# A hybrid transformer layer on one core: the Hyena filter's norm as a factor per channel, taps' sums from summed weights, and w_down's products of the FFN by halves of the columns

## The chip, the core and the metric

The kernel runs on one core of a Trainium2 chip. The core has a matmul engine (PE, with PEld for its weight loads), a vector engine (DVE), a scalar engine (ACT), a general engine (POOL), and SP, which here only issues transfers. The metric is the device time of one execution in microseconds; smaller is better. Products are kept near float32 by splitting every operand into a high and a low part and adding three matmuls (`mm3`); each split costs one ACT cast and one subtraction on DVE or POOL.

## The reference

Two layers over a stream x (512 tokens, width 1024) and a context stream (256 tokens). Each layer mixes x by attention, a Fourier mix and a Hyena long convolution, and then runs a gated FFN with a short convolution. In layer 0 the context is updated too. The parts that the change touches:

```python
def hyena_filter(L, w1, b1, fr1, w2, b2, fr2, w3):
    ...
    h = jnp.sin(fr1 * (z @ w1 + b1))
    h = jnp.sin(fr2 * (h @ w2 + b2))
    h = h @ w3                                   # L x 512: forward and backward taps
    h_fwd, h_bwd = h[:, :256] * decay, h[:, 256:] * decay
    two = jnp.concatenate([h_fwd, zeros, h_bwd[:0:-1]], axis=0)
    return two / jnp.sum(jnp.abs(two), axis=0, keepdims=True)

def hyena_longconv(u, filt, bias):               # by FFT of length 2L
    return irfft(rfft(u) * rfft(filt)) + u * bias

def hyena_mix(p, conv_w, conv_b, filt, bias):
    x0, x1, v = jnp.split(dwconv3(p, conv_w, conv_b), 3, axis=-1)
    return x0 * hyena_longconv(x1 * v, filt, bias)

def conv_ffn(h, w_up, w_c, b_c, w_down):
    gate, val = jnp.split(dwconv3(h @ w_up, w_c, b_c), 2, axis=-1)
    return (jax.nn.silu(gate) * val) @ w_down    # 2816 -> 1024
```

## The kernel before

The program is written as Python generators that a small list scheduler interleaves (`go` runs the main stage, `add` puts side work into lanes, `pump` steps side work by its due time, with costs such as `C512` and waits from the table `Z`). A framework then orders the instructions of each engine; that order is fixed in the program. On each engine instructions run strictly in order, and a wait holds up all that stand behind it.

**Hyena filters.** There are three: `c` (context, layer 0), `x0` and `x1` (x in layers 0 and 1). All three are side work: `c` runs in the first 45 us beside the loads of w_mod, and `x0` and `x1` run between about 45 and 245 us beside the input projections. `filter_taps` makes two sines (`sine`, tiles `taps`, `sn`) and then, for each tile of 128 taps, one product with w3 into PSUM, the multiplication by `decay` (`dec`), an absolute value (`fab`), a running sum of it on POOL, and sum and difference of the forward and backward halves (`fsd`), which are split into `sd`. At the end two matmuls with ones add the norm over all taps (line 792), and `inv` is its reciprocal, 128x256. `filter_spectrum` multiplies each transformed block by `inv` (`keo`), and adds and subtracts to make `K`, which goes to DRAM. `hyena` later multiplies the spectra and transforms back.

**FFN of x** (`ffn_x`). 22 column tiles m of w_up. Each takes seven products of half size (a Strassen-like scheme: `first` makes two, `rest` five; 84 matmuls of 256 columns). `prep` loads w_up (tiles `r`), POOL forms four differences (`tt`), and ACT and DVE split them (`Wh`, `Wl`, `w`). The convolution (`ft`), silu and the gate's product give `gT`, one tile per m. The m's go in nine groups of two and a last group of four. While group i runs, after its first m, `ffn_down` adds the products of group i−1 with w_down: it loads two row tiles of w_down, 128x1024 each (`Wr`, two buffers), splits them, makes 12 matmuls of 512 columns for each of the four token tiles into one PSUM tile of 1024 columns (`pw`, two buffers), and DVE adds that to `y` (line 1228; ACT copies it in the first group). The last group also does the norm and the residual (`tail`, `residual`, `norm_pre`).

```python
                if i and j == 0:
                    yield from self.ffn_down(l, st, g, groups[i - 1], i == 1)
```

In the rows below, `pn` and `pw` are PSUM tiles, `h` parts of the normed x, `Wh`/`Wl` split weights, `gT` split gates, `p`/`nmax` the attention's exponentials and row maxima, `rd_y` a reciprocal root for a norm.

## Time and profile before

| | |
|---|---|
| median of three runs (lowest, highest) | 1776.45 us (1773.36, 1780.07) |
| the profiled execution, its span | 1779.94 us, 1778.2 us |
| busy: PE, DVE, ACT, POOL | 1645.9, 1428.7, 932.4, 690.6 us |
| mean granted PE clock | 0.973 |
| context filter; filters of x; FFN of x, layer 0; FFN of x, layer 1 | about 10–42, 45–245, 700–1080, 1395–1774 us |

A page of the profile shows one execution. Busy times are shares of the span, so an average over stages with different limits; what a change in one stage is worth must be read from that stage. A row of a timeline gives start, duration, engine, line, operation, tiles, and in brackets how long the engine had stood idle and what released it. PE's matmuls are pipelined: a matmul of 256 columns is shown with 0.28 us, and one starts every 0.12 us.

### The profile page before, as it was taken

Reading aid. Unit: us, or ns where it says so; the run is one execution under the profiler, and the core shown is the slowest. Engines: PE = TensorE matmul, PEld = TensorE weight load, DVE = VectorE, ACT = ScalarE, POOL = GpSimd, SP = SyncE. Lnnn points to the kernel's source line nnn. Section 1 sums busy time; section 2 is a strip of 40 time slices with the busy share of each in tenths; the row PEclk is TensorE's granted clock in tenths of the full one; section 3 lists DMA queues with packets and bytes.
Section 4 is the critical chain, followed back from the end, with each engine's and each line's share of the span. In section 5 each row is a group of like instructions: output and inputs, shape, how many; then the busy total and the mean of one; then the engine's idle time right before and its main releaser. Section 6 shows DMA issues by size and latency. Waiting matters only on the chain. (4 is left out here: it accounts for less than half of the span.)

```text
span 1778.2 us, 27879 instructions
## 1 busy us (share of the span) xinstructions
PE 1645.9 (93%) x10534; PEld 1401.5 (79%) x10534; DVE 1428.7 (80%) x2291; ACT 932.4 (52%) x1741; POOL 690.6 (39%) x515
## 2 busy tenths in 40 slices
...
GB/s 348 121 60 147 93 236 273 224 13 139 166 252 227 229 151 83 83 119 85 106 142 84 95 184 314 201 175 119 1 48 83 131 145 105 97 105 87 125 64 119
DMA packets 70003, 248.01 MB, mean 139 GB/s; under 512 B 8111, under 2 KB 9647, under 8 KB 69868
## 3 DMA queue, kind: packets, MB, share of 16 engines
...
## 5 line engine op out<-in xcount | busy, mean ns | idle before, releaser
L196 PE MATMUL pn<-h,Wh 128*128 128x256 f32 x1328 | 376.4, 286 | 9.6 <-ACT Wh L181 3.4
L198 PE MATMUL pn<-h,Wl 128*128 128x256 f32 x1328 | 372.3, 284 | 10.0 <-DVE Wl L182 9.9
L197 PE MATMUL pn<-h,Wh 128*128 128x256 f32 x1328 | 374.0, 283 | 1.7 <-POOL h L182 1.7
L196 PEld LDWEIGHTS pn<-h,Wh 128*128 128x128 f32 x1328 | 252.7, 191 | 22.0 <-issue 4.8
L198 PEld LDWEIGHTS pn<-h,Wl 128*128 128x128 f32 x1328 | 251.7, 191 | 14.7 <-DVE Wl L182 12.1
L197 PEld LDWEIGHTS pn<-h,Wh 128*128 128x128 f32 x1328 | 253.5, 191 | 6.2 <-POOL h L182 2.4
L181 ACT CAST Wh<-Wr 128x1024 fp32r<-128x1024 f32 x118 | 122.7, 1048 | 139.1 <-PE pn L197 44.7
L182 DVE TENSOR_TENSOR Wl<-Wr,Wh 128x1024 fp32r<-128x1024 f32 x89 | 130.0, 1468 | 54.0 <-ACT Wh L181 46.4
L1302 POOL TENSOR_TENSOR tt<-r,r 128x512 f32<-128x512 f32 x44 | 73.2, 1664 | 236.4 <-DMA r<-w_up 223.4
L196 PE MATMUL pw<-Wh,gT 128*128 128x512 f32 x352 | 137.4, 403 | 9.0 <-ACT gT L181 3.8
L197 PE MATMUL pw<-Wl,gT 128*128 128x512 f32 x352 | 138.1, 395 | 3.3 <-DVE Wl L182 3.3
L198 PE MATMUL pw<-Wh,gT 128*128 128x512 f32 x352 | 137.9, 396 | 1.8 <-DVE gT L182 1.7
L181 ACT CAST Wh<-tt 128x1024 fp32r<-128x1024 f32 x88 | 90.8, 1048 | 81.8 <-PE pn L197 39.0
L182 DVE TENSOR_TENSOR Wl<-tt,Wh 128x1024 fp32r<-128x1024 f32 x88 | 121.0, 1394 | 12.3 <-ACT Wh L181 10.0
L1361 POOL TENSOR_TENSOR ft<-ft,ft 128x512 f32<-128x512 f32 x44 | 70.7, 1608 | 133.5 <-DVE ft L658 94.8
L1228 DVE TENSOR_TENSOR y<-y,pw 128x1024 f32<-128x1024 f32 x82 | 99.3, 1213 | 18.1 <-PE pw L198 18.0
L182 POOL TENSOR_TENSOR h<-tf,h 128x256 fp32r<-128x256 f32 (+1 forms) x40 | 35.0, 893 | 183.3 <-ACT h L181 182.0
L182 POOL TENSOR_TENSOR Wl<-Wr,Wh 128x1024 fp32r<-128x1024 f32 x29 | 72.6, 2508 | 59.6 <-ACT Wh L181 59.2
L1304 POOL TENSOR_TENSOR tt<-r,tt 128x512 f32<-128x512 f32 x44 | 75.8, 1722 | 47.6 <-DVE Wl L182 47.6
L656 ACT ACTIVATE ft<-C,vec 128x512 f32<-128x512 f32 x88 | 68.7, 811 | 36.7 <-DVE C L1351 27.4
L196 PE MATMUL pw<-h,Wh 128*128 128x256 f32 (+1 forms) x224 | 76.1, 340 | 12.7 <-DVE y L1228 2.6
L294 PE MATMUL pn<-wm,cpad 128*32 128x256 f32 x768 | 70.3, 427 | 16.8 <-DMA wm<-w_mod 16.2
...
## 6 DMA issues: line engine op xcount, KB each, us to landing
wm<-w_mod SPq DMA_DIRECT2D x96, 512.0 KB, 5.0
r<-w_up SPq DMA_DIRECT2D x90, 512.0 KB, 3.7
Wr<-w_down SPq DMA_DIRECT2D x66, 512.0 KB, 4.2
L<-w_up SPq DMA_DIRECT2D x44, 512.0 KB, 4.4
Wr<-w_out SPq DMA_DIRECT2D x24, 512.0 KB, 3.6
Wr<-w_in_t SPq DMA_DIRECT2D x16, 512.0 KB, 4.5
dft<-hdft_x POOLq DMA_DIRECT2D x16, 512.0 KB, 4.4
Wr<-w_in_c SPq DMA_DIRECT2D x12, 512.0 KB, 3.6
```

Source lines behind the costliest of these rows:

```text
L181: r = nc.scalar.copy(hi, src)
L182: (el or nc.vector).tensor_tensor(lo, src, f32(hi), op=ALU.subtract)
L196: nc.tensor.matmul(ps, l[0], r[0], start=first, stop=False, **kw)
L197: nc.tensor.matmul(ps, l[0], r[1], start=False, stop=False, **kw)
L198: nc.tensor.matmul(ps, l[1], r[0], start=False, stop=last, **kw)
L294: nc.tensor.matmul(ps[32 * g : 32 * g + 32, cs], self.cpad[:, q % 2 * 4 + g, :], w[:, g, :], start=q % 2 == 0, stop=q % 2 == 1, skip_group ...
L656: nc.scalar.activation(dst, ps, AF.Identity, scale=w1, bias=b)
L1228: nc.vector.tensor_tensor(y, y, acc[t], op=ALU.add)
L1302: te.tensor_tensor(half(t13, 0), half(r[1], 0), half(r[0], 0), op=ALU.subtract)
L1304: te.tensor_tensor(half(t24, 0), half(r[1], 1), half(t13, 0), op=ALU.subtract)
L1361: nc.gpsimd.tensor_tensor(o[0], o[0], o[1], op=ALU.mult)
```

## The change

It has two parts.

*Filter.* w3's two halves become their sum and difference once (DVE, 64x256 each), so that the matmul gives sum and difference of the taps directly, and one multiplication by a decay of 256 columns makes `fsd`. The absolute values for the norm come from max(|sum|, |difference|) (ACT makes the absolute values, DVE the maximum, POOL adds 256 columns instead of 512). The norm is taken per channel as a column (two matmuls with one moving column each) and is no longer multiplied into the spectrum: `hyena` applies 1/norm as a factor per channel in its last step, and bias times norm in the step before. `K` comes straight from PSUM, with one ACT copy and two DVE steps. A sine scales by 1/2π in an ACT step with scale and bias, rounds in two DVE steps, and calls Sin with a scale.

*FFN of x.* `down_half` takes one half of w_down's columns for both k of a group: one load of 128x2x512, 24 matmuls into two PSUM tiles, each of which holds two token tiles, and two sums. `Z['HV']` says after which m of a group each half stands: the first half after the first m, the second after the second; in group 1 both after the first; in the last group after its second and its fourth m. `y` is now a tile for two token tiles and one half of the columns. The residual is written into `xr`, and in layer 0 the norm's result into two halves.

```diff
+Z = {'HV': [[[0], [1]], [[0, 1], []], [[], [0], [], [1]]], 'go_mod00': 1.0, ...}   (the other entries as before)
...
         for k in range(4):
-            src = x[:, (4 * b + k) * P : (4 * b + k + 1) * P]
+            src = x[b][:, k * P : (k + 1) * P] if isinstance(x, list) else x[:, (4 * b + k) * P : (4 * b + k + 1) * P]
...
         else:
-            self.nc.scalar.activation(n, x, AF.Copy, scale=r)
+            for d, v in zip(n, (x[:, 0:512], x[:, 512:1024])) if isinstance(n, list) else [(n, x)]:
+                self.nc.scalar.activation(d, v, AF.Copy, scale=r)
...
     def sine(self, a, ps, b, fr):
-        nc = self.nc
-        T = a.shape[1]
-        n = self.T(T, "sn", parts=64)
-        nc.vector.tensor_scalar(a, ps, b, fr, op0=ALU.add, op1=ALU.mult)
-        nc.vector.tensor_scalar(n, a, 1.0 / TWO_PI, ROUND, op0=ALU.mult, op1=ALU.add)
-        nc.vector.tensor_scalar(n, n, -ROUND, None, op0=ALU.add)
-        for c in (CW1, CW2):
-            nc.vector.scalar_tensor_tensor(a, n, -c, a, op0=ALU.mult, op1=ALU.add)
-        nc.vector.tensor_scalar(a, a, PI_LO, -PI_LO, op0=ALU.min, op1=ALU.max)
-        nc.scalar.activation(a, a, AF.Sin)
+        nc = self.nc
+        n = self.T(a.shape[1], "sn", parts=64)
+        nc.scalar.activation(a, ps, AF.Identity, scale=fr, bias=b)
+        nc.vector.tensor_scalar(n, a, ROUND, None, op0=ALU.add)
+        nc.vector.scalar_tensor_tensor(a, n, ROUND, a, op0=ALU.subtract, op1=ALU.subtract)
+        nc.scalar.activation(a, a, AF.Sin, scale=-2.0 * PI_LO)
...
+        nc.vector.tensor_scalar(hw[:, 2:4], hw[:, 2:4], 1.0 / TWO_PI, None, op0=ALU.mult)
+        nc.vector.tensor_tensor(hw[:, 0:2], hw[:, 0:2], hw[:, 2:4], op=ALU.mult)
+        ws, wd = w3[:, 0:256], w3[:, 256:512]
+        nc.vector.tensor_tensor(ws, ws, wd, op=ALU.add)
+        nc.vector.scalar_tensor_tensor(wd, wd, -2.0, ws, op0=ALU.mult, op1=ALU.add)
...
-                    nc.gpsimd.dma_start(win2, I["decay_" + st.name][t // 2])
-            win = win2[:, t % 2]
-            dec = self.T(512, "dec")
-            nc.vector.tensor_tensor(dec, ps, win, op=ALU.mult)
-            ab = acc if t == 0 else self.T(512, "fab")
-            nc.vector.scalar_tensor_tensor(ab, dec, -1.0, dec, op0=ALU.mult, op1=ALU.max)
+                    nc.gpsimd.dma_start(win2, I["decay_" + st.name][t // 2, :, :, 0:256])
+            f = self.half2("fsd")
+            nc.vector.tensor_tensor(f, ps.rearrange("p (s d) -> p s d", s=2), win2[:, t % 2].unsqueeze(1).broadcast_to([P, 2, 256]), op=ALU.mult)
+            if t == 0:
+                nc.vector.tensor_tensor(f[0:1, 0], f[0:1, 0], f[0:1, 1], op=ALU.add)
+                nc.scalar.activation(f[0:1, 1], f[0:1, 0], AF.Copy, scale=0.5)
+                nc.scalar.activation(f[0:1, 0], f[0:1, 0], AF.Copy, scale=0.5)
+            ab = self.T(256, "fab") if t else acc
+            fa = self.half2("fa")
+            nc.scalar.activation(fa, f, AF.Abs)
+            nc.vector.tensor_tensor(ab, fa[:, 0], fa[:, 1], op=ALU.max)
...
-            f = self.half2("fsd")
-            nc.vector.tensor_tensor(f[:, 0, :], dec[:, 0:256], dec[:, 256:512], op=ALU.add)
-            nc.gpsimd.tensor_tensor(f[:, 1, :], dec[:, 0:256], dec[:, 256:512], op=ALU.subtract)
...
-        for e in range(2):
-            nc.tensor.matmul(ps[:, 0:256], self.ones.broadcast_to([P, P]), acc[:, e * 256 : (e + 1) * 256], start=e == 0, stop=e == 1)
-        o["inv"] = inv = acc[:, 0:256]
-        nc.vector.reciprocal(inv, ps[:, 0:256])
-        nc.vector.tensor_scalar(inv, inv, 1.0 / st.T, None, op0=ALU.mult)
-        yield CF512, 3.0
+        for m in range(2):
+            nc.tensor.matmul(ps[:, m : m + 1], acc[:, m * P : (m + 1) * P], self.ones, start=True, stop=True)
+        nrm = self.small("fnorm", 4, 3)
+        nc.vector.tensor_scalar(nrm[:, 2:4], ps[:, 0:2], float(st.T), None, op0=ALU.mult)
+        nc.vector.reciprocal(nrm[:, 0:2], nrm[:, 2:4])
+        nc.vector.tensor_tensor(nrm[:, 2:4], nrm[:, 2:4], self.vec[l][:, V_HB : V_HB + 2], op=ALU.mult)
+        o["norm"] = nrm
+        yield 0.4, 3.0
...
-                eo = self.half2("keo")
-                nc.vector.tensor_tensor(eo, ps.rearrange("p (e d) -> p e d", e=2), inv.unsqueeze(1).broadcast_to([P, 2, 256]), op=ALU.mult)
-                nc.vector.tensor_tensor(Kt[:, s, 0, :], eo[:, 0], eo[:, 1], op=ALU.add)
-                self.kp = nc.gpsimd.tensor_tensor(Kt[:, s, 1, :], eo[:, s], eo[:, 1 - s], op=ALU.subtract).ins
+                eo = self.T(256, "keo")
+                nc.scalar.copy(eo, ps[:, 256:512])
+                nc.vector.tensor_tensor(Kt[:, s, 0, :], ps[:, 0:256], eo, op=ALU.add)
+                if s == 0:
+                    self.kp = nc.vector.tensor_tensor(Kt[:, 0, 1, :], ps[:, 0:256], eo, op=ALU.subtract).ins
+                else:
+                    self.kp = nc.vector.scalar_tensor_tensor(Kt[:, 1, 1, :], ps[:, 0:256], -1.0, eo, op0=ALU.mult, op1=ALU.add).ins
...
-                nc.vector.scalar_tensor_tensor(t_, u[m][:, par : st.T : 2], vec[:, V_HB + m : V_HB + m + 1], ps[:, m * H : (m + 1) * H], op0=ALU.mult, op1=ALU.add)
-                nc.vector.tensor_tensor(self.mixf(st, 6 + m)[:, par : st.T : 2], t_, st.x0[m][:, par : st.T : 2], op=ALU.mult)
+                nc.vector.scalar_tensor_tensor(t_, u[m][:, par : st.T : 2], nrm[:, 2 + m : 3 + m], ps[:, m * H : (m + 1) * H], op0=ALU.mult, op1=ALU.add)
+                nc.vector.scalar_tensor_tensor(self.mixf(st, 6 + m)[:, par : st.T : 2], t_, nrm[:, m : m + 1], st.x0[m][:, par : st.T : 2], op0=ALU.mult, op1=ALU.mult)
...
-            nc.vector.scalar_tensor_tensor(y[:, hs], y[:, hs], r, x[:, hs], op0=ALU.mult, op1=ALU.add)
+            if isinstance(y, list):
+                nc.vector.scalar_tensor_tensor(x[:, hs], y[h], r, x[:, hs], op0=ALU.mult, op1=ALU.add)
+            else:
+                nc.vector.scalar_tensor_tensor(y[:, hs], y[:, hs], r, x[:, hs], op0=ALU.mult, op1=ALU.add)
...
-        if begin and st is self.X:
-            st.y = [self.M("y", F32) for _ in range(st.NT)]
-        wd = {k: self.load_w(self.I["w_down"][l, k], el=nc.gpsimd if el else None) for k in ms}
+        if st is self.X:
+            ww = [[self.load_down(l, k, h) for k in (ms[0], ms[2])] for h in range(2)]
+            W = lambda k, h: tuple(v[:, (k - ms[0]) % 2] for v in ww[h][(k - ms[0]) // 2])
+            st.y = [[st.Y[h][t // 2][:, t % 2 * 512 : t % 2 * 512 + 512] for h in range(2)] for t in range(st.NT)]
+        else:
+            wd = {k: self.load_w(self.I["w_down"][l, k], el=nc.gpsimd if el else None) for k in ms}
+            W = lambda k, h: tuple(v[:, h * 512 : (h + 1) * 512] for v in wd[k])
...
             for k in ks:
-                self.mm3(acc[t, h], (g[k][:, 0, ts], g[k][:, 1, ts]), (wd[k][0][:, hs], wd[k][1][:, hs]), k == ms[0], k == ms[-1])
+                self.mm3(acc[t, h], (g[k][:, 0, ts], g[k][:, 1, ts]), W(k, h), k == ms[0], k == ms[-1])
...
                 if end:
-                    nc.vector.tensor_tensor(y[:, hs], y[:, hs], acc[t, h], op=ALU.add)
-                    self.sumsq_half(ss[t], y[:, hs], h)
-                    nc.gpsimd.tensor_tensor(y[:, hs], y[:, hs], st.G[1][:, hs], op=ALU.mult)
+                    v = y[h] if st is self.X else y[:, hs]
+                    nc.vector.tensor_tensor(v, v, acc[t, h], op=ALU.add)
+                    self.sumsq_half(ss[t], v, h)
+                    nc.gpsimd.tensor_tensor(v, v, st.G[1][:, hs], op=ALU.mult)
...
+    def load_down(self, l, k, h):
+        return self.load_w(self.I["w_down"][l, k : k + 2, :, h * 512 : (h + 1) * 512].rearrange("k p c -> p k c"), [P, 2, 512])
+    def down_half(self, l, st, g, ms, h):
+        nc = self.nc
+        if ms[0] == 0:
+            if h == 0:
+                st.Y = [[], []]
+            st.Y[h] = [self.M("y", F32) for _ in range(st.NT // 2)]
+        w = self.load_down(l, ms[0], h)
+        for i, y in enumerate(st.Y[h]):
+            ps = self.pw()
+            for t in range(2):
+                ts = slice((2 * i + t) * P, (2 * i + t + 1) * P)
+                for k in range(2):
+                    v = g[ms[k]]
+                    self.mm3(ps[:, t * 512 : t * 512 + 512], (v[:, 0, ts], v[:, 1, ts]), (w[0][:, k], w[1][:, k]), k == 0, k == 1)
+                yield 6 * C512, 0.0
+            if ms[0] == 0:
+                nc.scalar.copy(y, ps)
+            else:
+                nc.vector.tensor_tensor(y, y, ps, op=ALU.add)
...
-                if i and j == 0:
-                    yield from self.ffn_down(l, st, g, groups[i - 1], i == 1)
+                if i:
+                    for h in Z["HV"][1 if i == 1 else 2 if i == len(groups) - 1 else 0][j]:
+                        yield from self.down_half(l, st, g, groups[i - 1], h)
...
                 if last:
-                    nc.sync.dma_start(self.out[t], st.y[t])
+                    nc.sync.dma_start(self.out[t], xr)
                 else:
-                    nc.sync.dma_start(self.dr["x2"][t], st.y[t])
-                    n = self.norm_diag(st.y[t], xr) if Z["DG"][2] >> t & 1 else self.norm_pre(st.y[t], xr, False, RT)
+                    nc.sync.dma_start(self.dr["x2"][t], xr)
+                    n = self.norm_diag(xr, st.y[t]) if Z["DG"][2] >> t & 1 else self.norm_pre(xr, st.y[t], False, RT)
```

The framework's order moves with it. Three places:

On ACT, the start of layer 0's attention, where the last steps of the context's residual (`rd_y`, casts `Wh` of w_out tiles) stand beside the first exponentials `p`. Before:

```order
L1001 ACTIVATE p_3334,den_3335<-pw_3327,nmax_3332 128x768
L224 ACT_TABLE_LOAD
L224 ACTIVATE rd_y_3239<-ss_3043,rd_x_3237 128x1
L181 CAST Wh_4249<-Wr_4247 128x1024
L181 CAST Wh_4279<-Wr_4277 128x1024
L233 ACTIVATE junk_3310,ss_3044<-pn_3285 128x512
L224 ACTIVATE rd_y_3315<-ss_3044,rd_x_3313 128x1
L181 CAST Wh_4318<-Wr_4316 128x1024
L181 CAST Wh_4398<-Wr_4396 128x1024
L1001 ACT_TABLE_LOAD
L1001 ACTIVATE p_3344,den_3335<-pw_3337,nmax_3342 128x768
L1001 ACTIVATE p_3353,den_3335<-pw_3346,nmax_3351 128x768
```

and now:

```order
L222 ACT_TABLE_LOAD
L222 ACTIVATE rd_y_3238<-ss_3042,rd_x_3236 128x1
L1014 ACT_TABLE_LOAD
L1014 ACTIVATE p_3333,den_3334<-pw_3326,nmax_3331 128x768
L179 CAST Wh_4248<-Wr_4246 128x1024
L179 CAST Wh_4278<-Wr_4276 128x1024
L231 ACTIVATE junk_3309,ss_3043<-pn_3284 128x512
L222 ACT_TABLE_LOAD
L222 ACTIVATE rd_y_3314<-ss_3043,rd_x_3312 128x1
L179 CAST Wh_4317<-Wr_4315 128x1024
L1014 ACT_TABLE_LOAD
L1014 ACTIVATE p_3343,den_3334<-pw_3336,nmax_3341 128x768
```

The fourth cast stands behind the next exponentials now, and there are two more table loads.

On DVE, one pair of m's in the steady part of layer 1's FFN (`Wl<-Wr` is a w_down tile, `y` the sums). Before:

```order
L1349 TENSOR_TENSOR C_15955<-C_15955,pn_15970 128x256
L1351 TENSOR_TENSOR C_15926<-pn_15927,C_15926 128x256
L1352 TENSOR_TENSOR C_15955<-pn_15927,C_15955 128x256
L1326 TENSOR_TENSOR C_16130<-C_16130,pn_16132 128x256
L182 TENSOR_TENSOR Wl_16065<-Wr_16062,Wh_16064 128x1024
L182 TENSOR_TENSOR Wl_16071<-Wr_16068,Wh_16070 128x1024
```

and now:

```order
L1278 TENSOR_TENSOR y_14697<-y_14697,pw_15731 128x1024
L1278 TENSOR_TENSOR y_14698<-y_14698,pw_15745 128x1024
L180 TENSOR_TENSOR Wl_15872<-tt_15865,Wh_15871 128x1024
L1397 TENSOR_TENSOR C_15759<-pn_15760,C_15759 128x256
L1398 TENSOR_TENSOR C_15788<-pn_15760,C_15788 128x256
L180 TENSOR_TENSOR gT_15720<-ft_15712,gT_15720 128x512
L180 TENSOR_TENSOR w_15875<-r_15858,w_15875 128x512
L180 TENSOR_TENSOR Wl_15898<-Wr_15895,Wh_15897 128x1024
```

The two w_down tiles of a group stood together; now each stands alone, behind the two sums of the half before it.

On SP's queue, where the w_down loads stand between the w_up loads. Before:

```order
L189 DMA Wr_8637<-w_down 128x1024
L189 DMA Wr_8643<-w_down 128x1024
L1295 DMA r_8599<-w_up 128x1024
L1295 DMA r_8600<-w_up 128x1024
L1295 DMA r_8862<-w_up 128x1024
```

and now:

```order
L187 DMA Wr_8636<-w_down 128x2x512
L1341 DMA r_8599<-w_up 128x1024
L1341 DMA r_8809<-w_up 128x1024
L187 DMA Wr_8847<-w_down 128x2x512
L1341 DMA r_8810<-w_up 128x1024
```

The loads alternate now, one w_down tile for each m.

More of the change, by code (lines that the diff above doesn't have):

```diff
@@ L30 @@
 ROUND = 12582912.0
-CW1 = 6.28125
-CW2 = float(TWO_PI - CW1)
 PI_LO = 3.1415925
@@ L754, in filter_taps @@
         w1, w2, w3 = hw[0:33, 4:68], hw[:, 68:132], hw[:, 132:644]
+        nc.vector.tensor_scalar(hw[:, 2:4], hw[:, 2:4], 1.0 / TWO_PI, None, op0=ALU.mult)
[3 more added lines that the diff above has]
+        nc.vector.scalar_tensor_tensor(wd, wd, -2.0, ws, op0=ALU.mult, op1=ALU.add)
         src, w = zT, w1
         keep = self.M("taps", F32)
-        acc = keep[:, 0:512]
+        acc = keep[:, 0:256]
         for j in range(2):
@@ L770, in filter_taps @@
             if t % 2 == 0:
[L771 removed]
+                win2 = self.Ld(512, "win").rearrange("p (t d) -> p t d", t=2)
                 with self.behind_c() if st is self.X else nullcontext():
[L773 to L778 removed]
+                    nc.gpsimd.dma_start(win2, I["decay_" + st.name][t // 2, :, :, 0:256])
[9 more added lines that the diff above has]
+            nc.vector.tensor_tensor(ab, fa[:, 0], fa[:, 1], op=ALU.max)
             if t:
                 nc.gpsimd.tensor_tensor(acc, acc, ab, op=ALU.add)
[L781 to L783 removed]
             yield 0.0, Z["tp1"]
@@ L800, in filter_spectrum @@
         half = st.NT // 2
-        sd, inv = o["sd"], o["inv"]
+        sd = o["sd"]
+        keep["norm"] = o["norm"]
         for ft in range(half):
```

9 lines of the change are left out of this document (4 added, 5 removed).

## The prediction

> **What bounds the kernel now.** I read the page's first block, then a table of busy time by stage, then every pause of the matmul engine (PE) in order of time.
>
> ```profile
> PE 1645.9 (93%) x10534; PEld 1401.5 (79%) x10534; DVE 1428.7 (80%) x2291; ACT 932.4 (52%) x1741; POOL 690.6 (39%) x515
> 0.00:45.00 45.00, 28.77 (x186) 12.69 (x186) 21.97 (x62) 13.75 (x26) 12.75 (x21) 1.00 0.92 346
> 45.00:250.00 205.00, 189.39 (x992) 151.75 (x992) 165.70 (x331) 85.50 (x206) 85.50 (x92) 0.97 0.40 124
> 250.00:350.00 100.00, 84.22 (x593) 63.93 (x591) 69.30 (x153) 47.52 (x118) 14.88 (x19) 0.95 0.76 253
> 740.00:900.00 160.00, 148.24 (x969) 133.63 (x968) 141.12 (x184) 94.35 (x151) 89.39 (x54) 0.98 0.36 112
> 900.00:1060.00 160.00, 155.82 (x1086) 142.59 (x1085) 144.18 (x161) 83.65 (x131) 80.89 (x54) 1.00 0.36 111
> 1480.00:1750.00 270.00, 266.43 (x1840) 245.88 (x1840) 251.56 (x278) 144.09 (x225) 136.18 (x82) 1.00 0.33 103
> ```
>
> After the stretch and its length stand the busy times of PE, PEld, DVE, ACT and POOL, then clock, DMA share and GB/s. PE is the bound, and no change to DVE or ACT is worth more than PE's pauses in its stage: 16.2 us in the start, 15.6 in 45–250 (where the Hyena filters of both layers run), 15.8 in 250–350, 11.8 and 4.2 in layer 0's FFN of x, 3.6 in the steady part of layer 1's. DVE is close behind PE in the FFN (251.6 of 270 us), so its lateness makes the pauses. These are the pauses that count (start, duration, instruction, in brackets the pause and its releaser):
>
> ```profile
> 18.54 1.11 PE L760 MATMUL pn<-taps,hw 64*64 64x256 f32 x2 [5.97 <-ACT taps L729]
> 114.33 0.35 PE L196 MATMUL pw<-h,Wh 128*128 128x256 f32 x1 [1.19 <-DVE rs_y L216]
> 141.81 0.47 PE L196 MATMUL pw<-h,Wh 128*128 128x512 f32 x1 [2.15 <-DVE v L658]
> 241.23 0.50 PE L196 MATMUL pn<-fd,f 128*128 128x512 f32 x1 [1.78 <-DVE cw L182]
> 350.07 0.79 PE L994 MATMUL pw<-KDup,Q 128*128 128x512 f32 x1 [6.78 <-ACT p L1001]
> 787.18 0.50 PE L197 MATMUL pw<-Wl,gT 128*128 128x512 f32 x1 [2.48 <-DVE Wl L182]
> 820.62 0.73 PE L196 MATMUL pw<-Wh,gT 128*128 128x512 f32 x2 [1.93 <-ACT gT L181]
> 892.19 1.22 PE L196 MATMUL pw<-Wh,gT 128*128 128x512 f32 x2 [2.21 <-ACT Wh L181]
> 912.74 0.38 PE L198 MATMUL pn<-h,Wl 128*128 128x256 f32 x1 [0.64 <-DVE Wl L182]
> 916.21 0.39 PE L198 MATMUL pn<-h,Wl 128*128 128x256 f32 x1 [0.80 <-DVE Wl L182]
> 1097.86 1.12 PE L361 MATMUL pn<-ident,xr 128*128 128x128 f32 x4 [1.77 <-ACT xr L379]
> 1476.88 0.38 PE L198 MATMUL pn<-h,Wl 128*128 128x256 f32 x1 [1.94 <-DVE Wl L182]
> ```
>
> **The change, part by part.** The profiled execution took 1779.94 us (span 1778.2), 3.5 above the median 1776.45; I work out a difference and take it from the median.
>
> Durations in the filter (ns, minimum/median/maximum):
>
> ```profile
> L723 DVE TENSOR_SCALAR taps<-pn,hw x6: 535/794/802, 11.4 to 170.4; 64x512 f32<-64x512 f32 x4, 64x256 f32<-64x256 f32 x2
> L724 DVE TENSOR_SCALAR sn<-taps x6: 278/409/419, 16.2 to 172.9; 64x512 f32<-64x512 f32 x4, 64x256 f32<-64x256 f32 x2
> L727 DVE SCALAR_TENSOR_TENSOR taps<-sn,taps x12: 406/673/686, 16.8 to 176.2; 64x512 f32<-64x512 f32 x8, 64x256 f32<-64x256 f32 x4
> L729 ACT ACTIVATE taps<-taps x6: 416/624/633, 18.1 to 179.2; 64x512 f32<-64x512 f32 x4, 64x256 f32<-64x256 f32 x2
> L778 DVE SCALAR_TENSOR_TENSOR fab<-dec x7: 673/691/1231, 31.0 to 221.0; 128x512 f32<-128x512 f32 x7
> L782 DVE TENSOR_TENSOR fsd<-dec x10: 404/412/2485, 26.8 to 221.7; 128x256 f32<-128x256 f32 x10
> L783 POOL TENSOR_TENSOR fsd<-dec x10: 724/744/1227, 26.3 to 221.9; 128x256 f32<-128x256 f32 x10
> L808 DVE TENSOR_TENSOR keo<-pn,taps x10: 676/682/692, 37.9 to 242.3; 128x512 f32<-128x512 f32 x10
> L794 DVE RECIPROCAL taps<-pn x3: 1748/1750/1757, 35.7 to 230.6; 128x256 f32<-128x256 f32 x3
> 33.76 1.86 PE L792 MATMUL pn<-taps,ones 128*128 128x256 f32 x4
> 136.85 1.03 PE L792 MATMUL pn<-taps,ones 128*128 128x256 f32 x4
> 35.46 0.60 PE L315 MATMUL pn<-ident,mods 128*128 128x128 f32 x4
> ```
>
> *A, the start (filter of the context).* PE stands 5.97 us for the first sine. Of the six DVE steps of a sine, two stay (like L724 and one L727) and one moves to ACT; four of 256 elements go, and DVE no longer interleaves them with the norms: 0.28+0.41+0.41+0.28 = 1.4 us sooner. The norm's ones-products, 1.86 us, become two matmuls with one moving column. None like it is in the trace; it costs over nothing and below the 0.60 of the four small ones at L315, and I take 0.4, so 1.4 is saved. PE hardly pauses between 18.5 and 42 us, so both count: −2.8. Ends: 0, if the w_mod transfers (0.92 of the DMA engines busy) end the stage anyway, and −7.4.
>
> *B, the filters of x, in 45–250.* DVE loses, for the two filters together: four sines at 0.79+0.41+0.41+2×0.67+0.41 = 3.4 us, against 1.1 left: 9.2; eight tiles of taps, 0.69 each (the larger absolute value against the maximum of halves, L782's size, stays): 5.5; reciprocal and scaling of 256 columns, 2.0 each: 4.1; eight spectrum blocks, 0.68+0.41 against two of 0.41: 2.2; and it gains 2×1.1 of preparing the weights (two tiny steps, two of 256). Net −19 of 165.7 us. POOL loses eight subtractions of 0.74, eight of K like them and half of six sums twice as wide, near 16 of 85.5. ACT gains four affine steps and eight absolute values of 0.62 and eight copies of half the width, taken at 0.4, +10.6 on 85.5 of 205 us: covered, since ACT is busy 42% there; without that cover the casts behind them would be late by one step, 0.6 us. PE itself saves 2×(1.03−0.4) = 1.3. Of the three pauses in the fence that DVE ends (5.1 us) I take half. B = −3.9; ends +2 (each absolute value in front of a cast that PE waits for, 0.6 at three places) and −10, two thirds of the stage's 15.6. The later products with the factor fold into steps that exist: nothing.
>
> *C, the attention's start.* Rows of ACT before the pause at 350:
>
> ```profile
> 342.32 0.29 ACT L224 ACTIVATE rd_y<-ss,rd_x 128x1 f32<-128x1 f32 x1
> 343.83 1.04 ACT L181 CAST Wh<-Wr 128x1024 fp32r<-128x1024 f32 x1 [1.22 <-DMA Wr<-w_out]
> 346.67 1.04 ACT L181 CAST Wh<-Wr 128x1024 fp32r<-128x1024 f32 x1 [1.79 <-DMA Wr<-w_out]
> 347.73 1.28 ACT L1001 ACT_TABLE_LOAD   x1
> 349.03 0.90 ACT L1001 ACTIVATE p<-pw,nmax 128x768 f32<-128x768 f32 x1
> 341.40 0.39 PE L994 MATMUL pw<-KDup,Q 128*128 128x512 f32 x1
> ```
>
> In the new order the exponentials stand ahead of the last of these casts, so they no longer queue behind a late w_out transfer. Two more table loads are paid: one ahead of the first exponential, under products already queued, and one ahead of rd_y. So rd_y ends at 342.3+1.3+0.3 = 343.9, the cast at 344.9, the load at 346.2, and the exponential starts there, not at 349.03: −2.8. Ends: 0, and −6.8. After the pause a matmul of 512 columns takes 0.79 us where it took 0.39 before it. The Trainium skill (TensorE: Matmul & The Clock Gate, "What's actually happening") says that PE's clock halves after an idle window of about 3.4 us; the trace agrees at this pause. By that rule a rest of 4.0 us still costs the slow stretch, and a rest below the window would be worth about 2 us more, which the sum leaves out.
>
> *D, layer 0's FFN (740–1060, 15.9 us of pauses).* PE's work stays, and so does that of DVE's splits and sums (four sums of 1024 per group). What moves is when: before, both w_down tiles of a group must be split by the group's fourth matmul, and four sums follow on two PSUM tiles; now one tile serves 24 matmuls, the next is due one m later, and two sums fit two PSUM tiles. The pauses on w_down's products quoted (2.48, 1.93, 2.21) make 6.6; I take 4.6 of them, since gT can still be late. Of those on the up-products (0.64, 0.80) I take 1. Two more table loads of 1.28 come in, half of one exposed: +0.6. D = −5.0; ends +3 (both loads exposed) and −15.9.
>
> *E, the end of layer 0.* The norm writes two halves instead of 1.15 us at once, and the first transposes need one: half of the 1.77 goes, −0.7; ends 0 and −1.8.
>
> *F, layer 1's FFN.* Of 1.94 at 1476 and the 3.6 us of the steady part I take 2.5; ends +2 (L1228's sums later than now) and −5.5.
>
> *G, given back.* In 250–350 PE waits for weights in transit:
>
> ```profile
> PEld pn L294 <- DMA wm<-w_mod: 7.5, 9, 1.5
> L181 ACT CAST Wh<-Wr 128x1024 fp32r<-128x1024 f32 x118 | 122.7, 1048 | 139.1 <-PE pn L197 44.7 <-PE pw L198 43.3 <-PE pw L197 33.6
> Wr<-w_down SPq DMA_DIRECT2D x66, 512.0 KB, 4.2
> ```
>
> Arriving 6.7 us sooner (A and B) brings it to transfers less ready; with DMA at 0.76 I give a third back, +2.2; ends 0 and +6.7.
>
> Sum: −2.8−3.9−2.8−5.0−0.7−2.5+2.2 = −15.5, and 1776.45−15.5 = 1761.0.
>
> **Rivals.** *1. The FFN's pauses move and don't go.* DVE has 251.6 us of work for 270, and spreading removes none of it; another split is then late in the same place. A, B, C and G stay, −7.3: 1769.2, no difference that can be told (about 0.5%, 8.9 us, is what a measurement of this kernel tells from none). For it speaks that the up-products' pauses name DVE too; against it, that the largest three are on w_down's products.
>
> *2. Slower: w_down's halves land late.* A tile is now two pieces of 2 KB per partition, of a row of 4. The load stays 512 KB, 4.2 us today, and sits on SP's queue between the w_up loads; in the casts' row no DMA is among the leading releasers, so today it is covered. If a landing outgrows that cover by 0.6 us, PE pays 0.6 for each of the 36 loads in the loop: +21.6, with A, B, C and G 1790.8. It decides from 0.45 us, where 16.2 outweigh those 7.3 by the 8.9 named above. Against it: DMA is at 0.33–0.36 there. The Trainium skill (DMA: Bandwidth & Descriptors, the table at its head) sets the least piece for full rate at 512 B, which would make this case void; no run here has shown it yet.
>
> *3. All of it.* If DVE's 19 us in the filters and the spread end nearly every pause they touch, A and B together reach −12, C −5 with the clock, D −12, F −5, −34 in all: 1742.5.
>
> **How the numbers follow.** Forecast 0.60, rival 1 0.23, rival 2 0.07, rival 3 0.10. The forecast's own range is 1752 to 1767; to hold 8 in 10 it goes to rival 3's middle and past rival 1: 1744 to 1775. Faster by over 0.5% (below 1767.6): forecast, rival 3 and little of rival 1, 0.70; within: 0.23; slower 0.07.
>
> **What would show it.** Right: the first sine's pause below 5 us; L792's group gone; exponentials starting sooner behind the last context residual; in 740–1060 PE idle under 11 us and no pause over 1.5 us on w_down's products. Wrong: PE idle near 16 us there with the pauses at splits of w_up (rival 1); casts of w_down released by DMA (rival 2); PE's pauses in 45–250 released by ACT, which is B's other end; the stage 250–350 longer by what was won before it, which would make G too small.

## The result, and the profile after

Thirteen runs of the changed kernel gave a median of 1770.74 us (1766.34 to 1777.10), thirteen of the kernel before 1782.12 (1773.36 to 1786.30). The ratio is 0.9936, 95% interval 0.9921 to 0.9951: faster by 0.64%, some 11.4 us, where 1761.0 stood against 1776.45, 15.5 us. Run again later, the same kernel gave 0.9933 (0.9910 to 0.9956). The profiled execution took 1770.96 us (span 1769.2).

The first block of the changed kernel's page, its stretches at the cuts of the prediction (PE, PEld, DVE, ACT, POOL busy, clock, DMA share, GB/s), and two groups of the page:

```profile
PE 1640.4 (93%) x10534; PEld 1400.9 (79%) x10534; DVE 1391.0 (79%) x2269; ACT 949.8 (54%) x1787; POOL 672.2 (38%) x495
0.00:45.00 45.00, 29.67 (x186) 13.22 (x186) 16.38 (x57) 17.89 (x37) 11.83 (x22) 1.00 0.98 361
45.00:250.00 205.00, 191.04 (x1011) 154.39 (x1012) 144.02 (x328) 99.50 (x237) 67.10 (x75) 0.96 0.38 120
250.00:350.00 100.00, 85.39 (x588) 65.49 (x587) 66.92 (x143) 50.15 (x119) 12.87 (x15) 0.92 0.73 247
740.00:900.00 160.00, 143.48 (x917) 129.96 (x916) 138.64 (x179) 90.28 (x144) 83.67 (x51) 0.95 0.32 101
900.00:1060.00 160.00, 158.72 (x1128) 146.75 (x1126) 146.89 (x169) 87.87 (x139) 85.81 (x55) 1.00 0.38 122
1480.00:1750.00 270.00, 267.10 (x1830) 245.56 (x1830) 243.26 (x284) 142.11 (x228) 136.53 (x83) 1.00 0.31 100
L179 ACT CAST Wh<-Wr 128x1024 fp32r<-128x1024 f32 x118 | 123.5, 1050 | 137.3 <-PE pn L195 63.1
Wr<-w_down SPq DMA_DIRECT2D x66, 512.0 KB, 3.9
```

DVE lost 21.7 us and POOL 18.4 in 45–250, ACT gained 14.0, near the 19, 16 and 10.6 forecast. PE's idle time in 740–1060 is 16.5 + 1.3 = 17.8 us, not under 11. These are PE's pauses that answer to those quoted before:

```profile
16.92 1.11 PE L762 MATMUL pn<-taps,hw 64*64 64x256 f32 x2 [4.18 <-ACT taps L725]
139.84 0.76 PE L194 MATMUL pw<-h,Wh 128*128 128x512 f32 x1 [2.49 <-DVE fnorm L801]
235.24 0.35 PE L194 MATMUL pn<-sd,dft 128*128 128x256 f32 x1 [1.79 <-ACT V L179]
346.31 0.80 PE L1007 MATMUL pw<-KDup,Q 128*128 128x512 f32 x1 [5.17 <-ACT p L1014]
760.51 1.07 PE L194 MATMUL pw<-Wh,gc 128*128 128x512 f32 x2 [2.25 <-ACT Wh L179]
777.54 0.62 PE L195 MATMUL pw<-Wl,gT 128*128 128x512 f32 x1 [1.95 <-DVE Wl L180]
817.41 0.39 PE L194 MATMUL pn<-h,Wh 128*128 128x256 f32 x1 [3.06 <-DVE C L1398]
846.67 3.57 PE L361 MATMUL pn<-dg,y 128*128 128x128 f32 x15 [4.35 <-DVE dg L348]
884.24 0.39 PE L194 MATMUL pn<-h,w 128*128 128x256 f32 x1 [1.80 <-ACT C L1391]
1471.69 0.38 PE L196 MATMUL pn<-h,Wl 128*128 128x256 f32 x1 [2.33 <-DVE Wl L180]
```

In layer 0's FFN the old pauses on w_down's products (2.48, 1.93, 2.21) are down to 1.95, and others have come: context products (`gc`), the sums `C`, and the context's transposes (`dg`), which stand 24 rows sooner in PE's order.

One profile is one execution, and the experiments gave eleven more of the layer, many with the same instructions over long stretches. Lengths in us from event to event: (1) start to the first transposes with a diagonal, (2) to the Fourier weights' products, the filters of x, (3) to the end of PE's pause at the attention, (4) to layer 0's first gate tile (cast of `gT`), (5) to the thirteenth, (6) to the first w_mod product behind that FFN, (7) to layer 1's Fourier weights, (8) to layer 1's first gate tile, (9) to the last matmul.

| | 1 | 2 | 3 | 4 | 5 | 6 | 7 | 8 | 9 |
|---|---|---|---|---|---|---|---|---|---|
| before | 56.8 | 179.2 | 114.0 | 377.2 | 203.7 | 137.2 | 145.0 | 219.4 | 335.7 |
| changed | 56.6 | 174.8 | 114.8 | 378.4 | 209.0 | 133.2 | 143.2 | 217.1 | 332.1 |
| changed, again | 56.0 | 170.7 | 114.4 | 378.4 | 210.1 | 134.9 | 143.2 | 218.7 | 333.9 |
| filter part alone | 52.7 | 172.1 | 114.3 | 378.4 | 205.9 | 136.5 | 143.6 | 221.7 | 339.7 |
| FFN part alone | 54.7 | 178.7 | 118.2 | 377.6 | 209.3 | 134.8 | 144.4 | 218.3 | 332.8 |
| halves without spread | 56.6 | 170.6 | 114.1 | 377.6 | 206.4 | 138.8 | 147.0 | 217.1 | 348.7 |
| context's transposes later | 53.7 | 170.8 | 113.0 | 377.1 | 211.5 | 133.1 | 151.4 | 217.1 | 335.3 |
| spread in part | 56.4 | 170.6 | 114.8 | 378.3 | 209.2 | 142.3 | 145.0 | 217.2 | 336.4 |
| changed, no low part | 56.9 | 170.4 | 116.6 | 379.1 | 193.4 | 131.7 | 150.2 | 219.2 | 331.4 |
| before, no low part | 54.5 | 176.7 | 114.3 | 378.3 | 199.1 | 138.8 | 142.6 | 217.3 | 333.7 |
| five splits on POOL | 54.1 | 172.2 | 114.5 | 377.2 | 218.1 | 131.7 | 148.0 | 218.9 | 334.2 |
| ten splits on POOL | 53.9 | 171.7 | 116.4 | 378.5 | 215.7 | 149.3 | 143.3 | 218.5 | 333.9 |
| roots on DVE | 53.3 | 172.6 | 116.8 | 377.9 | 207.8 | 133.5 | 144.3 | 220.6 | 335.4 |

### The profile page after: what moved, and what is told of

It is laid out like the page before. It is cut to its first block, busy times and chain, and to the rows that moved or that the text cites. A ratio compares the mean times of both kernels' runs of the same rounds, so it can differ in the third digit from the quotient of the medians.

```text
span 1769.2 us, 27894 instructions
## 1 busy us (share of the span) xinstructions
PE 1640.4 (93%) x10534; PEld 1400.9 (79%) x10534; DVE 1391.0 (79%) x2269; ACT 949.8 (54%) x1787; POOL 672.2 (38%) x495
## 5 line engine op out<-in xcount | busy, mean ns | idle before, releaser
L1348 POOL TENSOR_TENSOR tt<-r,r 128x512 f32<-128x512 f32 x44 | 66.0, 1501 | 260.7 <-DMA r<-w_up 224.8
L180 DVE TENSOR_TENSOR Wl<-Wr,Wh 128x1024 fp32r<-128x1024 f32 x89 | 121.5, 1367 | 53.2 <-ACT Wh L179 52.7
L180 DVE TENSOR_TENSOR Wl<-tt,Wh 128x1024 fp32r<-128x1024 f32 x88 | 129.8, 1495 | 7.5 <-ACT Wh L179 7.5
L1407 POOL TENSOR_TENSOR ft<-ft,ft 128x512 f32<-128x512 f32 x44 | 66.6, 1513 | 145.0 <-DVE ft L657 78.6
L180 POOL TENSOR_TENSOR h<-tf,h 128x256 fp32r<-128x256 f32 (+1 forms) x40 | 40.3, 1028 | 177.0 <-ACT h L179 177.0
L1350 POOL TENSOR_TENSOR tt<-r,tt 128x512 f32<-128x512 f32 x44 | 83.9, 1907 | 13.5 <-DVE Wl L180 13.5
L1278 DVE TENSOR_TENSOR y<-y,pw 128x1024 f32<-128x1024 f32 x64 | 77.3, 1212 | 7.8 <-PE pw L196 7.7
```

Source lines behind the costliest of these rows:

```text
L180: (el or nc.vector).tensor_tensor(lo, src, f32(hi), op=ALU.subtract)
L1278: nc.vector.tensor_tensor(y, y, ps, op=ALU.add)
L1348: te.tensor_tensor(half(t13, 0), half(r[1], 0), half(r[0], 0), op=ALU.subtract)
L1350: te.tensor_tensor(half(t24, 0), half(r[1], 1), half(t13, 0), op=ALU.subtract)
L1407: nc.gpsimd.tensor_tensor(o[0], o[0], o[1], op=ALU.mult)
```

## The experiments

**The two parts by themselves.** The first is the kernel before with the filter's edits, the second with the FFN's.

> The filter part alone on the kernel before. Theory (the two parts act apart): the filters of x end about 4 us sooner, most of that goes back to w_mod transfers before 335 us, the attention's start pause is 1 to 2 us shorter, so layer 0's FFN of x starts 2 to 3 us sooner, and layer 1's inverse transforms give about 2 us more: 4 to 5 us less in all, ratio 0.9972 to 0.9978; both FFNs keep their lengths (354.3 and 307.6 us) within 1 us. Rival (the filter's gain is all given back and only the FFN counts): within 1.5 us of before.

> The FFN part alone on the kernel before. Theory: up to layer 0's FFN nothing moves (within 0.5 us); that FFN is as long as before or 1 us longer, with a pause of PE over 3 us at the context's transposes, which stand 24 matmuls sooner here; layer 1's FFN is 3 us shorter; 2 to 5 us less in all, ratio 0.9972 to 0.9989. Rival (layer 0's FFN won nothing because the filter part brought its work there late): layer 0's FFN is 4 to 5 us shorter here, without that pause, and the total 7 to 9 us less.

```diff
 # filter alone: sine, filter_taps, filter_spectrum, hyena as in the diff of the change
 # FFN alone:    down_half, load_down, Z['HV'], y by halves, residual into xr
```

Filter alone: ratio 0.9979 (0.9963 to 0.9995), −3.7 us, near what was expected; but columns 1 and 2 show 11 us and not 4, and layer 1's FFN, whose code is the old one, took 4 us longer. FFN alone: 0.9996 (0.9980 to 1.0012), less than expected. Its pause at the context's transposes came (4.28 us), and column 9 was 2.9 shorter. But layer 0's FFN (columns 5 and 6) was 3.2 us longer, where at most 1 was expected, and column 3, which should not have moved, was 4.2 us longer.

The parts alone sum to 4.4 us (about ±4), the whole gives 11.4. The profiled execution of the filter alone has 4.8 us more of matmuls at half speed in layer 1's FFN: they cost 8.7 us there and 3.9 in the kernel before. (This cost, here and below, is worked out from the traces: the time beyond the usual step of a matmul of the same shape, over matmuls with no pause ahead that took more than 1.6 times that step.) The clock of its first 60 us was 0.94, and rows of ACT and DVE stand in another order there. Whether the order causes it, and the rest, stays open.

**Halves without the spread.**

> The changed kernel with both halves of w_down behind the first m of every group, so halves without the spread. Theory (the spread makes layer 1's gain and layer 0's new pause): no pause over 1.5 us at the context's transposes, layer 0's FFN 1 to 3 us shorter than in the changed kernel's 355.2, layer 1's FFN back to about 307 from 304.5; total within 2 us of the changed kernel. Rival (the halves' form makes it, one w_down tile for 24 matmuls): layer 1's FFN stays at 304 to 305 and the total is 2 us below the changed kernel's.

```diff
-Z = {'HV': [[[0], [1]], [[0, 1], []], [[], [0], [], [1]]], ...}
+Z = {'HV': [[[0, 1], []], [[0, 1], []], [[0, 1], [], [], []]], ...}
```

Ratio 1.0038 (1.0023 to 1.0052), some 18 us above the changed kernel by the ratios. Column 9 is 348.7, with 19.2 us of pauses where the changed kernel has 10.3; eight executions of the changed order lie between 332.1 and 336.4. So in layer 1 halves need the spread, and more strongly than either expectation had it: both behind one m are worse than the old form (335.7). In layer 0, column 5 fell by 2.6, and the context's transposes still waited 1.58.

**The context's transposes later.**

> The changed kernel with the context's transposes in layer 0's FFN due 6 us later in the planner (third entry of TC 16 for 10); the two square roots keep their separate table loads. Theory (PE waits there only because the transposes stand early in its order): the pause of 4.35 us falls below 1 us, layer 0's FFN is 350 to 352 us long where the changed kernel's took 355.2, and the total is 3 to 4.5 us below the changed kernel's, ratio to before 0.991. Rival 1 (DVE has no room there, the pause comes back at another split or sum): 354 to 356 us, total as the changed kernel's. Rival 2 (the additional table loads on ACT make DVE late, whatever PE does): the pause moves to products behind the gT that ACT casts late, and at most 1.5 us is won.

```diff
-Z = {..., 'TC': [50.0, 10.0, 10.0], ...}
+Z = {..., 'TC': [50.0, 10.0, 16.0], ...}
```

Ratio 0.9974 (0.9957 to 0.9991). The pauses at the transposes are gone and others stand there; two of them, PE's in layer 0 of this kernel:

```profile
840.30 0.38 PE L196 MATMUL pn<-h,Wl 128*128 128x256 f32 x1 [1.80 <-DVE Wl L180]
857.98 0.39 PE L194 MATMUL pn<-h,Wh 128*128 128x256 f32 x1 [2.77 <-ACT C L1393]
```

Column 5 is 211.5, not shorter, and column 7 grew by 8, with two waits for w_mod transfers in it (4.62 and 3.17). The theory fell; rival 1 of this expectation held for the stage, and the total is above the changed kernel's.

**The spread left out where the context's tail runs.**

> The changed kernel with the spread left out of layer 0's first groups alone: there, up to group 4, both halves of w_down stand behind the group's first m, while the context's tail runs beside them; the rest as in the changed kernel. From the first gate tile's cast in layer 0 to the thirteenth it took 203.7 and 205.9 us with the old products, 209.0, 209.3 and 211.5 with the spread, 206.4 without the spread. Theory (the spread collides with the context's tail in the first half of this FFN and wins behind it): 206 us or less for that stretch here, the second half as in the changed kernel, total 2 to 3 us below the changed kernel's, ratio to before 0.992. Rival (the pauses are set by the engines' work, not by where the halves stand): 209 to 211 us again, and the total as the changed kernel's.

```diff
-for h in Z["HV"][1 if i == 1 else ...][j]:
+for h in Z["HV"][1 if i == 1 or (l == 0 and i <= 4) else ...][j]:
```

Ratio 0.9978 (0.9960 to 0.9996). Column 5 stayed at 209.2, and column 6 was 9 us longer. That theory fell too.

**DVE's share, taken away.** The product with w_down's low part stays, but reads the high part.

> The changed kernel without the low part of w_down in both FFNs of x: the high part stands in for it, so PE's matmuls and transfers stay and DVE loses 22 subtractions of 1.4 us, 31 us, in each layer. Theory (DVE's lateness makes PE's pauses in the FFN): layer 0's FFN loses half or more of its 20 us of pauses, so 8 to 12 us, layer 1's 3 to 6 us of its 10; total 11 to 18 us below the changed kernel's. Rival (the pauses come from chains across ACT, POOL and PE that DVE's load doesn't lengthen): each layer within 3 us, total within 5.

> The kernel before without the low part of w_down in both FFNs of x (the high part stands in for it; matmuls and transfers stay). Theory (both forms of the w_down products are equal where DVE isn't late): the stretch to the thirteenth gate tile falls from 203.7 to 191 to 195 us as in the changed form (193.4), layer 1's FFN from 335.7 to 331 to 332; total 15 to 20 us below before, and what is left to the changed form without the low part (0.9843 of before) is the filter's 7 to 9 us. Rival (the spread saves PE something else than DVE's lateness): layer 1's FFN stays at 334 or more.

```diff
     def load_down(self, l, k, h):              # the kernel before: the same in ffn_down
-        return self.load_w(self.I["w_down"][l, k : k + 2, ...], [P, 2, 512])
+        r = self.tl([P, 2, 512], F32, "Wr")
+        self.nc.sync.dma_start(r, self.I["w_down"][l, k : k + 2, ...])
+        w = self.tl([P, 2, 512], F32R, "Wh")
+        self.nc.scalar.copy(w, r)
+        return w, w
```

Changed form: 0.9843 (0.9818 to 0.9867), 16.3 us below the changed kernel's median in the same runs. Old form: 0.9942 (0.9924 to 0.9960), 10 us below before, less than the 15 to 20 expected. So relieved, the two forms lie 17.6 us apart by the ratios, not 7 to 9: the theory that they are then equal fell. The stretches of columns 5 and 9, in the order before, changed, changed without the low part, before without it:

```profile
727.24:930.94 203.70, 188.35 (x1235) 170.47 (x1234) 180.38 (x228) 117.35 (x187) 110.67 (x67) 0.97 0.36 112
1432.56:1768.30 335.74, 324.62 (x2203) 293.89 (x2202) 305.46 (x350) 178.71 (x285) 174.72 (x107) 1.00 0.33 106
...
724.68:933.68 209.00, 189.29 (x1224) 172.22 (x1224) 182.47 (x227) 117.78 (x187) 111.47 (x67) 0.95 0.34 108
1427.16:1759.27 332.11, 321.82 (x2204) 292.53 (x2202) 297.71 (x350) 176.45 (x285) 173.51 (x107) 1.00 0.33 107
...
723.05:916.48 193.43, 182.28 (x1204) 166.90 (x1204) 161.12 (x214) 114.99 (x182) 104.23 (x67) 0.96 0.36 115
1417.49:1748.85 331.36, 322.56 (x2203) 293.05 (x2202) 264.31 (x328) 178.87 (x285) 163.95 (x107) 1.00 0.34 107
...
723.87:922.94 199.07, 185.80 (x1224) 169.40 (x1223) 168.93 (x215) 119.78 (x188) 103.91 (x67) 0.97 0.37 114
1421.62:1755.29 333.67, 324.15 (x2203) 294.20 (x2202) 263.38 (x328) 178.89 (x285) 163.40 (x107) 1.00 0.33 106
```

In layer 0's first half 21.4 us less of DVE shortened the changed form by 15.6, of which 8.5 are pauses of PE (19.7 to 11.2); the stretch also holds 20 fewer matmuls. The old form lost 4.6 us for 11.5 less of DVE (199.1, where 191 to 195 were expected), and of its 13.2 us of pauses ACT ends 12.1. So in the changed form w_down's low part holds that stretch up, and in the old form it does so much less. The edit takes away a wait as well as work: no product waits for that split any more, and the runs don't tell the two apart. In layer 1, 33.4 us less shortened the changed form by 0.8, less than the 3 to 6 expected. The relieved forms took 331.4 and 333.7 there, a difference that single executions can't tell, since the changed order alone spreads over 332.1 to 336.4.

**The changed kernel again.**

> The changed kernel once more, to see which stage lengths repeat and to compare on this chip. All theories: ratio to before 0.992 to 0.996. From the first context-weighted transposes (50 to 57 us) to the Fourier weights' products it took 170.6 to 174.8 us in four executions of the same instructions, where the granted clock was 1.00 and 0.97: theory (the difference is the clock) 170 to 175 us, the longer the lower the clock.

The filters of x in three executions, before, changed, changed again:

```profile
56.81:236.04 179.23, 170.18 (x900) 138.17 (x901) 146.01 (x265) 70.03 (x162) 74.37 (x79) 0.98 0.32 99
...
56.65:231.48 174.83, 168.44 (x900) 137.95 (x901) 123.21 (x253) 82.50 (x190) 61.81 (x65) 0.97 0.32 95
...
56.04:226.75 170.71, 164.12 (x900) 134.25 (x901) 123.25 (x253) 82.19 (x190) 63.05 (x65) 1.00 0.32 98
```

The same instructions took 174.8 us at 0.97 and 170.7 at 1.00; DVE, ACT and POOL agree to 1.3 us. Matmuls at half speed cost 6.6 us in the one and 2.4 in the other. So the difference lies in PE's clock, as expected, and two single profiles can't size a gain below some 4 us per stage.

**A pause's price, by itself.**

> Only matmuls of 256 columns in dense blocks of 10 to 13 us, between them a pause of PE of ten lengths from about 0.7 to 4.5 us (one ACT step of 256 to 3840 elements), twelve times each; the layer is left out and the output is zero. Theory (a pause of 1.5 to 3 us is followed by half speed in some cases only, by where it falls in a fixed window of time): none slow below about 1 us, all slow from some 3.5 us, a share in between that grows with the pause, and each slow stretch lasts 3 to 5 us and costs 1.5 to 2.3 us. Rival (a fixed length decides): none slow below one length and all above it.

```diff
+for k in range(84 + (q * 37) % 29):
+    nc.tensor.matmul(ps[...], wt, dst[:, 0:256], start=True, stop=True)
+nc.scalar.copy(s_, ps[:, 0:4])
+nc.scalar.activation(dst[:, 0:n], src[:, 0:n], AF.Identity, bias=s_[:, 0:1])
```

A block counts as slow if it took over 1 us longer than 0.1172 us for each matmul. After pauses of 0.8 to 1.65 us, 0 of 36 were slow; of 1.9 to 2.7 us, 40 of 59; of 3.1 and 3.8 us, 23 of 24. A slow block took 1.2 to 1.5 us longer than a fast one of its length, and in five of twelve cases after 3.8 us up to 2.4. PE's rows of two blocks behind the same pause, and of one behind a short pause:

```profile
706.03 4.28 PE L1652 MATMUL ps<-dst,wt 128*128 128x256 f32 x21 [2.07 <-ACT dst L1655]
...
872.39 7.81 PE L1652 MATMUL ps<-dst,wt 128*128 128x256 f32 x63 [2.07 <-ACT dst L1655]
...
104.78 5.42 PE L1652 MATMUL ps<-dst,wt 128*128 128x256 f32 x43 [1.65 <-ACT dst L1655]
```

Each row is what the view shows to its window's end: 0.20 us for a matmul behind the first pause, 0.12 behind the others. The theory held; a fixed length doesn't decide. A rule that fits can be read from the same trace. Cut the time into windows of 3.4134 us from one starting point: a block is slow where PE stood for 1.85 us or more within a single window, and all 119 blocks come out right. The window's length, start and limit are fitted to these same blocks, but no other length from 2 to 7 us (beyond 0.05 us from this one) leaves fewer than 8 wrong, and the pause's length alone leaves 20. The Trainium skill (TensorE: Matmul & The Clock Gate, "What's actually happening") describes a window of about 3.4 us that runs free of the program, which agrees with the chance; its table has the clock fall after an idle window of that length, and here 1.9 us was enough in most cases.

**DVE's work moved to POOL.**

> The changed kernel with five of layer 0's w_down subtractions (the second half of each of the first five groups) on POOL, 2.5 us each there, in place of DVE, 1.4 us. The run without the low part showed DVE's lateness in this FFN's first half: 14 us less of DVE gave 209 to 193 us there. Theory (POOL has room, 111 of 209 us): DVE loses 7 us, the stretch from the first to the thirteenth gate tile takes 202 to 206 us, total 3 to 6 us below the changed kernel's, ratio to before 0.990 to 0.992. Rival (POOL's gate product is in the chain to gT, and 2.5 us in front of it make gT late): 208 us or more, the total as the changed kernel's or above.

> The same with all ten subtractions of the first five groups on POOL: DVE loses 14 us, POOL gains 25. Theory: 196 to 203 us for the stretch, total 6 to 10 us below the changed kernel's. Rival (POOL late): 209 us or more, with PE's pauses released by gT or POOL, the total above the changed kernel's.

```diff
+el = self.nc.gpsimd if l == 0 and k < 10 and h == 1 else None    # all ten: without h == 1
```

Ratios 1.0008 (0.9993 to 1.0023) and 1.0046 (1.0029 to 1.0063): both worse, as the rival had it, though mostly not where it said. With ten splits the largest pause of PE names DVE, not POOL:

```profile
853.80 0.58 PE L194 MATMUL pn<-h,Wh 128*128 128x256 f32 x1 [5.89 <-DVE C L1395]
```

Ten microseconds ahead of it DVE had stood 3.38 us for a root of the context's norm from ACT, and from there to that sum its rows follow one another without a pause. POOL ended 6.1 of the 25.1 us of pauses in column 5.

DVE was hardly relieved, either. With ten subtractions fewer, its durations in column 5 add up to 195.0 us, against 197.5 in the changed kernel. The trace shows why: its steps between tiles in SBUF (the on-chip memory beside PSUM) take longer while POOL runs. Of the changed kernel's 44 subtractions of 128x1024 in that stretch, the 20 with POOL idle took 1.20 to 1.23 us each; the 18 with POOL busy for most of the step took 1.21 to 2.33, 1.85 on average (1.93 with ten splits on POOL, up to 3.07). The sums `y`, which read PSUM, took 1.21 either way. Two DVE rows of the changed kernel and the POOL row beside the second:

```profile
806.11 1.21 DVE L180 TENSOR_TENSOR Wl<-tt,Wh 128x1024 fp32r<-128x1024 f32 x1
809.62 2.31 DVE L180 TENSOR_TENSOR Wl<-tt,Wh 128x1024 fp32r<-128x1024 f32 x1
...
809.10 1.75 POOL L1349 TENSOR_TENSOR tt<-r 128x512 f32<-128x512 f32 x1
```

**The roots of the context's tail on DVE.**

> The changed kernel with the four reciprocal roots of the context's tail in layer 0's FFN made by DVE alone (three Newton steps from an integer guess, as elsewhere in this kernel), so that ACT loads no table for Sqrt or back for Silu there: six loads of 1.28 us go, DVE gets some twelve more steps on one column. In the changed kernel one pair of these roots is split by a Silu, DVE stands 3.12 us for the second root, and PE 4.35 us at the transposes behind it. Theory (that stall of DVE, with the DVE work queued behind it, made this FFN's first half longer by 5 us): the stretch from the first to the thirteenth gate tile takes 200 to 205 us where the changed kernel's took 209.0 and 210.1, total 4 to 8 us below the changed kernel's, ratio to before 0.989 to 0.992. Rival (DVE's whole load sets the pauses and the stall fills itself elsewhere): 208 us or more and the total as the changed kernel's.

```diff
 def rstd(self, ss):
+    if self.newton:                                # in tail_c only
+        return self.rsqrt(ss[:, 0:1], D, ss[:, 1:2])
```

Ratio 0.9953 (0.9931 to 0.9974). Column 5 is 207.8, one to two below the changed kernel, and PE still stands at the transposes:

```profile
846.34 3.09 PE L364 MATMUL pn<-dg,y 128*128 128x128 f32 x16 [4.07 <-DVE dg L351]
```

So the table loads alone aren't the cause. The rival (DVE's whole load) is left, but no run shows it by itself. No version beat the changed kernel among those that compute the layer in full.

## Why the prediction was right, point by point

The side and the range held. The size missed by 4 us, with terms that err against each other: the measured 11.4 lies as far from the forecast's 15.5 as from rival 1's 7.3, so that only the stages tell the two apart. Measured are means from the table: for columns 1 to 4 three executions of the old filter against ten of the new; for 5 to 8 before and filter alone against changed, again and FFN alone; for 9 the same two against the eight executions with the changed order of that stage.

| term | forecast | measured |
|---|---|---|
| A, start (1) | −2.8 | −0.3 |
| B, filters of x (2) | −3.9 | −6.6 |
| C and G (3) | −0.6 | −0.5 |
| column 4 | 0 | +0.4 |
| D, layer 0's FFN (5 and 6) | −5.0 | +2.1 |
| E, its end (7) | −0.7 | −0.7 |
| column 8 | 0 | −2.5 |
| F, layer 1's FFN (9) | −2.5 | −3.5 |
| sum | −15.5 | −11.6, by the runs −11.4 |

**A.** The steps were right in the sine and wrong in what follows: the first sine's pause fell from 5.97 to 4.18 (forecast 1.4, measured 1.8). The product with a column took 0.87 us from start to start where 0.4 was taken, since PE ran at half speed there; in the filter alone, at full speed, it took 0.47. PE's rows of this stretch, changed and filter alone, the same instructions:

```profile
28.56 3.64 PE L292 MATMUL pn<-wm,cpad 128*32 128x256 f32 x32
32.13 1.01 PE L799 MATMUL pn<-ones,taps 128*128 128x1 f32 x4
...
25.19 1.93 PE L292 MATMUL pn<-wm,cpad 128*32 128x256 f32 x32
28.83 0.61 PE L798 MATMUL pn<-ones,taps 128*128 128x1 f32 x4 [1.71 <-POOL taps L788]
```

The stage's length went from 52.7 to 56.9 with the new filter and from 54.5 to 56.8 with the old. The gain is smaller than that. (The clock column reads 1.00 in both stretches; here the matmuls tell the state, not the column.)

**B.** The direction was right, the size too small, and the pauses that went are mostly not those named. Of the three (5.1 us, half of it taken), only the 1.19 is gone. The 2.15 is 2.49 now, behind the norm's own column (`fnorm`), and where the 1.78 stood, 1.79 stand ahead of another product. Smaller pauses went, and the stage's fell from about 9 us to between 6 and 7. PE's own work, forecast at 1.3 less, fell from 167.2 to 164.1 us at a clock of 1.00 (before without the low part, changed again). Of that 3.1 the ones-products explain about 1.2, and matmuls at half speed 1.7, which the clock column doesn't show. The mean cost of half speed in this stage is 5.7 us in the three old executions and 3.4 in the ten new ones; the forecast has no term for it.

**C and G.** Their sum came as forecast, their parts did not. ACT at the attention's start in the changed kernel:

```profile
341.46 0.29 ACT L222 ACTIVATE rd_y<-ss,rd_x 128x1 f32<-128x1 f32 x1
342.91 1.04 ACT L179 CAST Wh<-Wr 128x1024 fp32r<-128x1024 f32 x1 [1.15 <-DMA Wr<-w_out]
343.97 1.28 ACT L1014 ACT_TABLE_LOAD   x1
345.26 0.90 ACT L1014 ACTIVATE p<-pw,nmax 128x768 f32<-128x768 f32 x1
```

The chain of root, cast, load and exponential is the one forecast, and one cast still waits for w_out ahead of the exponentials. They start at 345.26, where 346.2 was worked out; but the stage itself began 4.6 us sooner here, and counted from its start they come at 113.8 us, before at 113.0. PE's pause was 6.5 to 7.0 us in three executions of the old order and 4.9 to 6.0 in ten of the new, so C gave 1.4 and not 2.8. What was given back is then some 0.9 and not 2.2, by difference, not by a row of its own. After the pause matmuls ran at half speed in every one of these. Column 3 moved less than its spread (113.0 to 118.2), so that the agreement of the sum is luck.

**D.** This step failed. It priced pauses that it took to go, by 4.6 + 1 us, with table loads at 0.6. The pauses on w_down's products did go (6.6 us to 1.95), but all of them stood in the first half, beside the context's tail, and column 5 grew by 4.7: there rival 1 was right. Spreading takes no work off DVE, and pauses came back elsewhere. PE stood 15.3 and 20.3 us in all with the old products, 19.7 to 21.6 with the new. The longest was 3.62 at most and is 4.28 to 4.43 now, and matmuls at half speed cost 6.3 and 3.9 us there, 6.7 to 9.9 here. The second half gave 2.6 (column 6), with no priced pause in it. What made the new order worse than the old in the first (203.7 and 205.9) isn't settled. With the transposes later it was 211.5, without the table loads 207.8, with the spread left out in these groups alone 209.2; without any spread it came to 206.4, near the old form. Without w_down's low part it was 193.4. Each edit also makes the framework order the rest of the stretch anew, so none of these takes one thing away alone.

**E** came as forecast by its pause: 1.77 us at the first transposes is 0.56 now. Column 7 itself spreads over 142.6 to 151.4 and says little. **F** came near, and no closer than the executions allow. The pause of 1.94 stayed (2.33), against the forecast; the stage came to 332.1 to 336.4 us, 334.2 on average, where before took 335.7 and the filter alone, in another order and with 4.8 us more of half speed, 339.7. Against before alone F is −1.5. Column 8, forecast at nothing, is −1.4 against before alone; the filter alone's 221.7 makes the rest.

**Rival 2** didn't come: w_down's halves land in 3.9 us (4.2 before) and no DMA leads the casts' releasers. The Trainium skill (DMA: Bandwidth & Descriptors, the table at its head) had it so with its least piece of 512 B. **Rival 3** didn't come: it needed −12 of A and B, −5 of C and −12 of D, and none came near.
